# A mixture-of-experts kernel: 32 places on four column tiles for the two least used experts, wider steps, and the least used expert inside the first

## The chip, the cores and the metric

The kernel runs on one NeuronCore of a Trainium2 chip. The metric is the device time of one execution in microseconds (us), the median of several. TensorE multiplies matrices, VectorE (DVE) and ScalarE (ACT) work on the results, SyncE (SP) issues the DMA transfers, and sixteen DMA engines move data from the main memory (HBM) to the core.

## The reference

Two decoder layers on 256 tokens of width 1024, in 32-bit floats. Each layer has four kinds of attention and then a channel mixer. Layer 0 has a dense one, layer 1 one of eight experts, of which each token uses two:

```
def swiglu(x, w1, w3, w2):
    return (jax.nn.silu(x @ w1) * (x @ w3)) @ w2

logits = (xf @ w_router).astype(jnp.float32)
top_logits, top_e = lax.top_k(logits, 2)
gates = jax.nn.softmax(top_logits, axis=-1)
# each expert e: y = swiglu(its tokens, w1[e], w3[e], w2[e]), D = 1024, D_FF = 3584
# out[token] += y * gate
```

An expert has three matrices of 1024 x 3584 words, 44 MB in all; eight experts are 352 MB, and all of it has to come from HBM in each execution.

## The kernel before

The program up to about 612 us (attention, layer 0) is the same in both kernels. After it come the eight experts, one behind the other. `ranks` sorts the experts 1 to 7 by how many tokens chose them; expert 0 of the reference has rank 0, and the numbers of the others (`ids`) go to SP's registers by `values_load` (L1032), since the addresses of their weights depend on them. "Expert r" below is the one of rank r. The order is `ORDER`, (0, 7, 1, 2, 6, 3, 4, 5).

**Two kinds of expert.** `Big` (ranks 0 to 4) has 128 places for tokens. Its weights are split: `split_unit` writes the high part `whi` on ScalarE (L100) and the rest `wlo` on VectorE (L108), 1024 columns at a time with five buffers of each, and `mm3` (L134 to L136) makes three matmuls of one. `Small` (ranks 5 to 7) has 64 places and plain 32-bit matmuls of the raw weights (L1159, L1184); two matmuls of 64 columns of the array each, for different columns of the weights, fill the array.

**Loads.** `load_raw` (L84) gives a buffer of 1 MB (128 x 2048 words) from a ring of 12 with four names (raw 4, side 3, post 3, early 2) and issues a DMA for it on SP's queue. SP issues in order, so a load waits for the one before it and for the buffer's last reader, twelve loads back. An expert is 42 such loads.

**Steps.** A `Big` takes D_FF in seven steps of 512 columns, a `Small` in 1024, 1024, 1024 and 512. One step of the loop in `experts_in` is: `up` with w1; in the middle of it (after four of eight row blocks) `turn` transposes the last step's result (L1115, or L1169); silu on ScalarE (L1240); `down` of the last step with w2; `up` with w3; and on VectorE the product with the gate (L1244, `stt` below). So the last step of an expert is turned and multiplied down inside the first step of the next one. `gather` brings an expert's tokens together (L1061 and after) in the middle of the expert before, and `put_back` adds the result to `h` (L1136 for Big, L1198 for Small, L1204). PSUM has four banks for `wk` (up, turn, gather, put_back) and four for `acc` (down).

A load of 1 MB has rows in HBM of 2 KB (a step of 512 columns of w1 or w3), 4 KB (1024 columns) or 8 KB (all w2).

## Time and profile before

| | before |
|---|---|
| median of 3 runs | 1553.82 us (1552.64 to 1554.4) |
| profiled execution, its own time | 1550.38 us |
| its span | 1548.5 us |
| mean granted clock of TensorE | .993 |
| TensorE busy | 1502.4 us, 97% |
| VectorE busy | 1000.8 us, 65% |
| ScalarE busy | 842.9 us, 54% |
| read from HBM | 454.42 MB |

The span runs from the first to the last instruction on the core, the own time has some 2 us around it. The first 612 us are attention and layer 0, and the eight experts take from there to about 1505 us, so the shares of the whole span are a mean over both; the views by stage, below, tell them apart.

### The profile page before, as it was taken

The numbers are of one execution on the slowest core, as the hardware profiler recorded it, in microseconds if no ns is written. First come the engines' busy times: TensorE is split into PE (matmuls) and PEld (weight loads), VectorE is DVE, ScalarE is ACT, GpSimd is POOL, SyncE is SP. The second block draws the span as 40 slices with busy tenths as digits, with TensorE's granted clock in tenths as the row PEclk, the third lists the DMA queues.
The fourth block names the chain that finished last, engine by engine and source line by source line (L and its number), as shares of the span: only waits on it lengthen the run. The fifth ranks groups of instructions, "written<-read, shape, count | busy, mean of one in ns | idle before, by whom it ended". The sixth has DMA issues, their size and how long they took to land. (4 is left out here: it accounts for less than half of the span.)

```text
span 1548.5 us, 19459 instructions
## 1 busy us (share of the span) xinstructions
PE 1502.4 (97%) x7104; PEld 1106.6 (71%) x7104; DVE 1000.8 (65%) x1330; ACT 842.9 (54%) x1166; POOL 17.9 (1%) x20
## 2 busy tenths in 40 slices
PE   8999999999999997999999999999999999999988
PEld 6877788888788776887446888886346888885336
DVE  7676654554786767987107889886117889885016
ACT  6656544444556565876116677775025777673014
POOL 1000000000010000000000000000000000000001
PEclk9999999999999998999999999999999999999998
DMA  8553655463254642999999999999999999999993
GB/s 275 176 189 123 223 181 200 165 215 137 97 166 167 233 150 73 400 396 340 408 406 398 396 397 398 394 353 363 399 404 396 398 398 395 384 335 373 397 391 110
DMA packets 167302, 456.80 MB, mean 295 GB/s; under 512 B 10720, under 2 KB 21792, under 8 KB 151072
## 3 DMA queue, kind: packets, MB, share of 16 engines
q1 hardware_dynamic: 167200, 455.50, 78.8%
q8 instruction: 57, 0.93, 0.2%
q14 instruction: 45, 0.37, 0.1%
HBM read 454.42 MB, written 1.05 MB: 294 GB/s over the span
## 5 line engine op out<-in xcount | busy, mean ns | idle before, releaser
L108 DVE TENSOR_TENSOR wlo<-raw,whi 128x1024 fp32r<-128x1024 f32 (+1 forms) x260 | 308.6, 1214 | 77.1 <-ACT whi L100 71.7
L100 ACT ACTIVATE whi<-raw 128x1024 fp32r<-128x1024 f32 (+1 forms) x260 | 264.2, 1050 | 118.8 <-PE acc L135 66.9
L134 PE MATMUL wk<-whi,xgh 128*128 128x512 f32 x560 | 221.2, 395 | 6.7 <-ACT whi L100 6.7
L136 PE MATMUL wk<-wlo,xgh 128*128 128x512 f32 x560 | 221.7, 396 | 0.6 <-DVE wlo L108 0.6
L135 PE MATMUL wk<-whi,xgl 128*128 128x512 f32 x560 | 219.7, 392 | 0.2 <-DVE xgl L130 0.2
L108 DVE TENSOR_TENSOR wlo<-post,whi 128x1024 fp32r<-128x1024 f32 x134 | 160.9, 1221 | 21.7 <-ACT whi L100 19.7
L108 DVE TENSOR_TENSOR wlo<-side,whi 128x1024 fp32r<-128x1024 f32 x134 | 160.1, 1221 | 22.3 <-ACT whi L100 20.1
L100 ACT ACTIVATE whi<-post 128x1024 fp32r<-128x1024 f32 x134 | 137.1, 1054 | 49.9 <-PE wk L135 30.6
L134 PE MATMUL acc<-whi,gh 128*128 128x512 f32 x392 | 154.7, 395 | 4.3 <-ACT whi L100 3.3
L135 PE MATMUL acc<-whi,gl 128*128 128x512 f32 x392 | 154.7, 395 | 0.0
L1244 DVE SCALAR_TENSOR_TENSOR sl<-sl,gs,wk 128x512 f32<-128x512 f32 (+1 forms) x47 | 34.3, 730 | 182.1 <-PE wk L1159 142.1
L100 ACT ACTIVATE whi<-side 128x1024 fp32r<-128x1024 f32 x134 | 138.2, 1055 | 21.5 <-PE acc L135 11.2
L136 PE MATMUL acc<-wlo,gh 128*128 128x512 f32 x392 | 144.8, 395 | 0.1
L134 PEld LDWEIGHTS wk<-whi,xgh 128*128 128x128 f32 x560 | 105.7, 189 | 30.6 <-ACT whi L100 9.4
L136 PEld LDWEIGHTS wk<-wlo,xgh 128*128 128x128 f32 x560 | 105.8, 189 | 24.9 <-DVE wlo L108 1.6
L135 PEld LDWEIGHTS wk<-whi,xgl 128*128 128x128 f32 x560 | 105.5, 188 | 22.3 <-DVE xgl L130 0.5
L108 DVE TENSOR_TENSOR wlo<-early,whi 128x1024 fp32r<-128x1024 f32 x72 | 85.7, 1221 | 7.9 <-ACT whi L100 6.9
L134 PEld LDWEIGHTS acc<-whi,gh 128*128 128x128 f32 x392 | 73.8, 188 | 23.6 <-ACT whi L100 5.0
L134 PE MATMUL wk<-whi,hTh 128*128 128x512 f32 x224 | 88.1, 393 | 1.0 <-ACT whi L100 1.0
L136 PE MATMUL wk<-wlo,hTh 128*128 128x512 f32 x224 | 87.4, 391 | 0.1
L135 PE MATMUL wk<-whi,hTl 128*128 128x512 f32 x224 | 87.2, 390 | 0.0
L136 PEld LDWEIGHTS acc<-wlo,gh 128*128 128x128 f32 x392 | 73.6, 188 | 18.1 <-DVE wlo L108 1.0
(397 smaller groups left out, 2314.0 us busy)
## 6 DMA issues: line engine op xcount, KB each, us to landing
raw<-in_moe_w_dram SPq DMA_DIRECT2D x112, 1024.0 KB, 12.7
side<-in_moe_w_dram SPq DMA_DIRECT2D x84, 1024.0 KB, 12.8
post<-in_moe_w_dram SPq DMA_DIRECT2D x84, 1024.0 KB, 12.6
early<-in_moe_w_dram SPq DMA_DIRECT2D x56, 1024.0 KB, 12.9
raw<-in_w_in_dram SPq DMA_DIRECT2D x20, 1024.0 KB, 6.2
raw<-in_ffn_w_dram SPq DMA_DIRECT2D x19, 1024.0 KB, 5.1
post<-in_ffn_w_dram SPq DMA_DIRECT2D x14, 1024.0 KB, 5.1
side<-in_ffn_w_dram SPq DMA_DIRECT2D x9, 1024.0 KB, 5.1
```

The costliest lines, as they stand in the source:

```text
L100: nc.scalar.activation(hi, v, AF.Copy)
L108: engine.tensor_sub(lo, v, hi.bitcast(FT))
L134: nc.tensor.matmul(ps, xh, wh, start=first, stop=False)
L135: nc.tensor.matmul(ps, xl, wh, start=False, stop=False)
L136: return nc.tensor.matmul(ps, xh, wl, start=False, stop=last)
L1244: nc.vector.scalar_tensor_tensor(sl[:, :n], sl[:, :n], now.gs, ps, op0=OP.mult, op1=OP.mult)
```

## The change

The ranks 6 and 7 get 32 places and four column tiles (`q` = 4) instead of two; rank 5 keeps 64. `Big` takes 1024 columns in a step (and 512 in the last), so that `up` fills two PSUM banks and w1 and w3 are read in rows of 4 KB. `Small` takes 2048 and then 1536 columns, with rows of 8 and 6 KB; the loads of the second step are 768 KB in a buffer of 1 MB, and what remains of w2 there comes as two DMAs of 512 KB in one buffer. The loop runs over a list of pairs (expert, step), `STEPS`: the two steps of expert 7 stand behind the first of expert 0, whose other three follow. `gather` is made two steps ahead. `sl`, `gh` and `gl` are twice as wide and have one buffer in place of two.

```diff
-N_BIG = 5
-ORDER = (0, 7, 1, 2, 6, 3, 4, 5)
+PLACES = (128, 128, 128, 128, 128, 64, 32, 32)
+STEPS = [(0, 0), (7, 0), (7, 1), (0, 1), (0, 2), (0, 3)] + [
+    (r, c) for r in (1, 2, 6, 3, 4, 5) for c in range(2 if PLACES[r] < 128 else 4)]
...
-                nc.vector.tensor_scalar(room[:, N_BIG:], room[:, N_BIG:], 64.0, None, op0=OP.add)
+                for r, n in enumerate(PLACES):
+                    if n < 128:
+                        nc.vector.tensor_scalar(room[:, r:r + 1], room[:, r:r + 1], 128.0 - n, None, op0=OP.add)
...
+                cols = [(0, 1024), (1024, 1024), (2048, 1024), (3072, 512)]
+
                 def __init__(self, r, got):
                     self.r, (self.x, self.ohT, self.gs) = r, got
-                    self.cols = [(c * 512, 512) for c in range(NFC)]
                     self.y = None
+
+                def banks(self, c):
+
+                    return [512] * (self.cols[c][1] // 512)
...
-                    ps = work()
+                    ps = [work() for _ in self.banks(c)]
                     src = of_expert(name, self.r).rearrange("(k p) n -> p k n", p=128)[:, :, c0:c0 + n]
                     for k, (wh, wl) in enumerate(weights(src, [128, KD, n])):
                         if between is not None and k == 4:
                             between()
-                        mm3(ps, self.x[0][:, k], self.x[1][:, k], wh, wl, k == 0, k == KD - 1)
+                        for f, p in enumerate(ps):
+                            fs = slice(f * 512, (f + 1) * 512)
+                            mm3(p, self.x[0][:, k], self.x[1][:, k], wh[:, fs], wl[:, fs], k == 0, k == KD - 1)
...
                 def turn(self, g, c):
-                    gh = mp.tile([128, 4, 128], FR, name="gh", tag="gh", bufs=2)
-                    gl = mp.tile([128, 4, 128], FR, name="gl", tag="gl", bufs=2)
-                    p = work().rearrange("p (a b) -> p a b", a=4)
-                    for j in range(4):
-                        nc.tensor.transpose(p[:, j], g[:, 256 * (j // 2) + j % 2:256 * (j // 2 + 1):2], ident)
-                    split_sb(gh, gl, p)
+                    gh = mp.tile([128, 8, 128], FR, name="gh", tag="gh")
+                    gl = mp.tile([128, 8, 128], FR, name="gl", tag="gl")
+                    for j0 in range(0, self.cols[c][1] // 128, 4):
+                        p = work().rearrange("p (a b) -> p a b", a=4)
+                        for j in range(4):
+                            o = 128 * j0 + 256 * (j // 2)
+                            nc.tensor.transpose(p[:, j], g[:, o + j % 2:o + 256:2], ident)
+                        split_sb(gh[:, j0:j0 + 4], gl[:, j0:j0 + 4], p)
                     return gh, gl
...
+                cols = [(0, 2048), (2048, 1536)]
+
+                def __init__(self, r, got, n):
                     super().__init__(r, got)
-                    self.cols = [(0, 1024), (1024, 1024), (2048, 1024), (3072, 512)]
+                    self.n, self.q = n, 128 // n
+
+                def banks(self, c):
+                    w = self.cols[c][1] // self.q
+                    return [min(512, w - o) for o in range(0, w, 512)]
+
+                def rows(self, u):
+                    return slice(u * self.n, (u + 1) * self.n)
...
-                    ps = work()[:, :n // 2]
+                    ps = [work()[:, :w] for w in self.banks(c)]
                     src = of_expert(name, self.r).rearrange("(k p) n -> p k n", p=128)[:, :, c0:c0 + n]
-                    m = CHUNK // n
                     for k in range(KD):
-                        if k % m == 0:
-                            raw = load_raw(src[:, k:k + m], [128, m, n])
+                        raw = load_raw(src[:, k:k + 1], [128, 1, n])
                         if between is not None and k == 4:
                             between()
-                        for u in range(2):
-                            nc.tensor.matmul(ps[64 * u:64 * u + 64], self.x[:, k],
-                                             raw[:, k % m, u * (n // 2):(u + 1) * (n // 2)],
-                                             start=k == 0, stop=k == KD - 1, skip_group_check=True)
+                        for f, p in enumerate(ps):
+                            for u in range(self.q):
+                                o = u * (n // self.q) + f * 512
+                                nc.tensor.matmul(p[self.rows(u)], self.x[:, k], raw[:, 0, o:o + p.shape[1]],
+                                                 start=k == 0, stop=k == KD - 1, skip_group_check=True)
...
+                    parts = []
+                    for u in range(self.q):
+                        for a in range(w // 256):
+                            r0 = c0 + u * w + a * 256
                             raw = load_raw(wd[r0:r0 + 256].rearrange("(p j) n -> p j n", j=2), [128, 2, D])
+                            parts += [(raw[:, j], 2 * a + j, u) for j in range(2)]
+                            self.multiply(gT, c, parts)
+                        if w % 256 and u % 2:
+                            raw = load_raw(None, [128, 2, D])
                             for j in range(2):
-                                for f in range(2):
-                                    nc.tensor.matmul(self.y[64 * f:64 * f + 64], gT[:, 2 * a + j, 64 * u:64 * u + 64],
-                                                     raw[:, j, f * 512:(f + 1) * 512],
-                                                     start=(c, u, a, j) == (0, 0, 0, 0),
-                                                     stop=(c, u, a, j) == (len(self.cols) - 1, 1, n // 512 - 1, 1),
-                                                     skip_group_check=True)
+                                r0 = c0 + (u + j) * w - 128
+                                nc.sync.dma_start(raw[:, j], wd[r0:r0 + 128])
+                            parts += [(raw[:, j], w // 128 - 1, u - 1 + j) for j in range(2)]
+                            self.multiply(gT, c, parts)
+
+                def multiply(self, gT, c, parts):
+                    w = D // self.q
+                    for raw, j, u in parts:
+                        self.left = getattr(self, "left", D_FF // 128) - 1
+                        for f in range(self.q):
+                            nc.tensor.matmul(self.y[self.rows(f)], gT[:, j, self.rows(u)],
+                                             raw[:, f * w:(f + 1) * w], start=self.left == D_FF // 128 - 1,
+                                             stop=self.left == 0, skip_group_check=True)
+                    parts.clear()
...
-                                               accum_out=sums[:, t, f:f + 1])
+                                               accum_out=sums[:, t, f:f + 1] if w == 512 else None)
...
+                places = [128] * N_EXP if base else PLACES
+                seq = STEPS if base == 0 else [(r, c) for r in range(N_EXP) for c in range(len(Big.cols))]
+                first = {}
+                for s, (r, c) in enumerate(seq):
+                    first.setdefault(r, s)
+                halves_ = [0]
+                made = {}
+
+                def make(r):
+                    n = places[r]
+                    got = gather(r, n, PLACES[r] if base else 0, halves_[0])
+                    if n == 128:
+                        halves_[0] ^= 1
+                        made[r] = Big(r, got)
+                    else:
+                        made[r] = Small(r, got, n)
+
+                def make_for(s):
+                    for r, f in first.items():
+                        if f and max(f - 2, 0) == s and r not in made:
+                            make(r)
+
+                make(seq[0][0])
...
-                for place in range(N_EXP):
-                    for c in range(len(now.cols)):
-                        ps = now.up("moe_w1", c, turn_last)
-                        n = now.cols[c][1] // (2 if isinstance(now, Small) else 1)
-                        sl = mp.tile([128, 512], FT, name="sl", tag="sl", bufs=2)
-                        nc.scalar.activation(sl[:, :n], ps, AF.Silu)
-                        if before_ is not None:
-                            before_[0].down(gT, before_[1])
-                        ps = now.up("moe_w3", c)
-                        nc.vector.scalar_tensor_tensor(sl[:, :n], sl[:, :n], now.gs, ps, op0=OP.mult, op1=OP.mult)
-                        if c == len(now.cols) // 2 and place + 1 < N_EXP:
-                            then = make(place + 1)
-                        if before_ is not None:
-                            finish_last()
-                        g, before_ = sl, (now, c)
-                    now = then
+                for s, (r, c) in enumerate(seq):
+                    now = made[r]
+                    ps = now.up("moe_w1", c, turn_last)
+                    sl = mp.tile([128, 1024], FT, name="sl", tag="sl")
+                    for f, p in enumerate(ps):
+                        nc.scalar.activation(sl[:, f * 512:f * 512 + p.shape[1]], p, AF.Silu)
+                    if before_ is not None:
+                        before_[0].down(gT, before_[1])
+                    elif len(seq) > 1:
+                        make_for(s)
+                    ps = now.up("moe_w3", c)
+                    for f, p in enumerate(ps):
+                        fs = slice(f * 512, f * 512 + p.shape[1])
+                        nc.vector.scalar_tensor_tensor(sl[:, fs], sl[:, fs], now.gs, p, op0=OP.mult, op1=OP.mult)
+                    if before_ is not None:
+                        make_for(s)
+                        finish_last()
+                    g, before_ = sl, (now, c)
```

SP's queue, where the experts' numbers come to it, first before. `DMA` rows are the loads, with the buffer's name and the transfer's shape; `TENSOR_LOAD ids` fetches an expert's number.

```order
L84 DMA side<-in_moe_w_dram 128x4x512 x2
L84 DMA raw<-in_w_out_dram 128x2x1024
L84 DMA raw<-in_moe_w_dram 128x4x512
...
L84 DMA post<-in_moe_w_dram 128x4x512
L84 DMA early<-in_moe_w_dram 128x4x512
L84 DMA post<-in_moe_w_dram 128x2048
L1032 TENSOR_LOAD ids
...
L84 DMA post<-in_moe_w_dram 128x4x512
L84 DMA early<-in_moe_w_dram 128x4x512
L84 DMA raw<-in_moe_w_dram 128x2048
```

The same place after the change:

```order
L86 DMA side<-in_moe_w_dram 128x2x1024 x2
L86 DMA raw<-in_w_out_dram 128x2x1024
L86 DMA raw<-in_moe_w_dram 128x2x1024
...
L86 DMA post<-in_moe_w_dram 128x2x1024
L86 DMA early<-in_moe_w_dram 128x2x1024
L86 DMA post<-in_moe_w_dram 128x2x1024
L1037 TENSOR_LOAD ids
...
L86 DMA raw<-in_moe_w_dram 128x2048
L86 ISA
L86 DMA side<-in_moe_w_dram 128x2048
```

Ten loads of expert 0 stood ahead of the numbers, now eight of them, its whole first step up; behind them came expert 0's further weights, and now come those of expert 7.

TensorE at the first matmuls of expert 7, before: the last `up` of expert 0 (`wlo`, `xgh`), then expert 7's first loads (`xe` are its tokens), the turn of expert 0's last step (`sl`), and its last down (`acc`).

```order
L136 MATMUL wk<-wlo,xgh 128x512
L1159 MATMUL wk<-raw,xe 64x512 x4
L1159 MATMUL wk<-side,xe 64x512 x4
L1115 MATMUL wk<-ident,sl 128x128 x4
L1159 MATMUL wk<-post,xe 64x512 x4
L1159 MATMUL wk<-raw,xe 64x512 x4
L134 MATMUL acc<-whi,gh 128x512
```

And after:

```order
L138 MATMUL wk<-wlo,xgh 128x512
L1189 MATMUL wk<-raw,xe 32x512 x4
L1189 MATMUL wk<-side,xe 32x512 x4
L1189 MATMUL wk<-post,xe 32x512 x4
L1189 MATMUL wk<-early,xe 32x512 x4
L1128 MATMUL wk<-ident,sl 128x128 x8
L1189 MATMUL wk<-raw,xe 32x512 x4
L1189 MATMUL wk<-side,xe 32x512 x4
L1189 MATMUL wk<-post,xe 32x512 x4
L1189 MATMUL wk<-early,xe 32x512 x4
L136 MATMUL acc<-whi,gh 128x512
```

Before, this place is behind expert 0's seventh step, now behind its first; eight loads with four matmuls each make one `up`, and the turn takes eight transposes.

VectorE between two steps of a Big, before (512 columns, expert 0), with `stt` at L1244 and `gl` at L130:

```order
L1244 SCALAR_TENSOR_TENSOR sl<-sl,gs,wk 128x512
L108 TENSOR_TENSOR wlo<-early,whi 128x1024
L108 TENSOR_TENSOR wlo<-raw,whi 128x1024 x2
L130 TENSOR_TENSOR gl<-wk,gh 128x512
L108 TENSOR_TENSOR wlo<-side,whi 128x1024 x2
```

And after, with `stt` at L1314 and `gl` at L132:

```order
L1314 SCALAR_TENSOR_TENSOR sl<-sl,gs,wk 128x512 x2
L1252 SCALAR_TENSOR_TENSOR h,sums<-h,wk 128x512
L110 TENSOR_TENSOR wlo<-raw,whi 128x1024 x2
L110 TENSOR_TENSOR wlo<-side,whi 128x1024 x2
L110 TENSOR_TENSOR wlo<-post,whi 128x1024
L132 TENSOR_TENSOR gl<-wk,gh 128x512 x2
```

The pieces of 512 columns stand in pairs now, once in 24 split units instead of once in 12.

## Rows read from the trace of the kernel before

In the timelines L134 to L136 are the matmuls of Big, L1159 and L1184 those of Small up and down, and L1115 is the turn of Big; a row of count x8 is one load of Small, in which each matmul has two records. In the windows the columns are: stretch, its length, busy time of PE, PEld, DVE, ACT and POOL, the granted clock, the share of DMA, and GB/s.

**Rows 1.** The page of the profiled execution, its first line.
```profile
span 1548.5 us, 19459 instructions
```

**Rows 2.** Busy time in us and records (x), by stage; clock, DMA share, GB/s.
```profile
612.00:730.00 118.00, 117.77 (x535) 96.46 (x534) 104.24 (x114) 92.11 (x98) 0.00 (x0) 1.00 0.98 373
730.00:818.00 88.00, 86.11 (x427) 35.92 (x426) 14.88 (x26) 11.79 (x19) 0.00 (x0) 1.00 0.98 388
818.00:1069.00 251.00, 248.76 (x1116) 200.82 (x1116) 214.39 (x218) 179.00 (x203) 0.00 (x0) 1.00 1.02 386
1069.00:1158.00 89.00, 85.71 (x422) 35.01 (x418) 14.41 (x25) 12.80 (x20) 0.00 (x0) 1.00 1.01 395
1158.00:1411.00 253.00, 250.40 (x1114) 201.91 (x1114) 214.37 (x215) 179.85 (x204) 0.00 (x0) 0.99 1.02 383
1411.00:1505.00 94.00, 87.49 (x423) 34.06 (x422) 12.69 (x20) 10.22 (x16) 0.00 (x0) 1.00 1.01 396
...
```

**Rows 3.** The same columns for short stretches inside the stages.
```profile
840.00:860.00 20.00, 20.00 (x92) 16.50 (x91) 18.06 (x18) 15.17 (x17) 0.00 (x0) 1.00 1.04 395
1040.00:1060.00 20.00, 20.00 (x91) 16.44 (x90) 17.55 (x17) 14.95 (x17) 0.00 (x0) 1.00 0.99 369
1100.00:1120.00 20.00, 20.00 (x96) 6.81 (x94) 0.75 (x1) 1.19 (x2) 0.00 (x0) 1.00 1.02 416
1114.00:1121.00 7.00, 7.00 (x36) 2.61 (x34) 0.75 (x1) 0.60 (x1) 0.00 (x0) 1.00 1.01 421
1160.00:1180.00 20.00, 18.30 (x70) 11.54 (x69) 12.05 (x17) 11.01 (x12) 0.00 (x0) 0.91 1.03 398
```

**Rows 4.** TensorE's timeline: start, length, line, operation, count, [idle before, releaser].
```profile
817.59 0.50 PE L134 MATMUL wk<-whi,xgh 128*128 128x512 f32 x1 [1.64 <-ACT whi L100]
...
839.55 0.63 PE L1115 MATMUL wk<-ident,sl 128*128 128x128 f32 x4
...
856.56 0.63 PE L1115 MATMUL wk<-ident,sl 128*128 128x128 f32 x4
...
1068.77 1.51 PE L1159 MATMUL wk<-post,xe 128*64 128x512 f32 x6
...
1181.86 0.63 PE L1115 MATMUL wk<-ident,sl 128*128 128x128 f32 x4
```

**Rows 5.** TensorE's timeline in an expert of 64 places, a load a row.
```profile
777.49 1.94 PE L1159 MATMUL wk<-early,xe 128*64 128x512 f32 x8
779.25 1.89 PE L1159 MATMUL wk<-raw,xe 128*64 128x512 f32 x8
```

**Rows 6.** TensorE's timeline: a gather's first and last rows, a put-back's, what follows.
```profile
675.61 0.40 PE L1061 MATMUL wk<-hsh,oh 128*128 128x512 f32 x1
...
679.00 0.46 PE L1068 MATMUL wk<-ident,xs 64*128 64x64 f32 x4
...
751.13 0.50 PE L1136 MATMUL wk<-yh,ohT 128*128 128x512 f32 x1
...
753.17 1.08 PE L1159 MATMUL wk<-post,xe 128*64 128x512 f32 x4
```

**Rows 7.** Waits of SP's queue, 590 to 625 us: total, times, longest.
```profile
SPq L1032 <- DVE ids L1012: 12.7, 1, 12.7
```

**Rows 8.** DMA issues, 616:617 and 1044:1069: count, KB, us to landing.
```profile
post<-in_moe_w_dram SPq DMA_DIRECT2D x1, 1024.0 KB, 5.1
...
side<-in_moe_w_dram SPq DMA_DIRECT2D x3, 1024.0 KB, 7.2
```

**Rows 9.** Groups of VectorE's instructions, 818 to 1069: busy, mean ns, idle before.
```profile
L108 DVE TENSOR_TENSOR wlo<-post,whi 128x1024 fp32r<-128x1024 f32 x42 | 50.0, 1220 | 1.5 <-ACT whi L100 1.5
...
L1244 DVE SCALAR_TENSOR_TENSOR sl<-sl,gs,wk 128x512 f32<-128x512 f32 x14 | 10.5, 747 | 17.2 <-PE wk L136 17.2
L130 DVE TENSOR_TENSOR gl<-wk,gh 128x512 fp32r<-128x512 f32 x13 | 8.9, 685 | 0.1
```

**Rows 10.** TensorE's timeline, the matmuls on the last expert load.
```profile
1502.60 1.89 PE L1184 MATMUL acc<-early,ge 128*64 128x512 f32 x8
```

More of the change, by code (lines that the diff above doesn't have):

```diff
@@ L1038, in of_expert, with gather @@
                 return I[name][0, bass.ds(expert[r], 1)].rearrange("e k n -> (e k) n")
-            def gather(r, place, base):
-                small = r >= N_BIG
-                n = 64 if small else 128
+            def gather(r, n, off, half):
+                small = n < 128
                 sr, gr = (slot, gate) if r == 0 else (slot_r, gate_r)
@@ L1077, in gather @@
                         ins = split_sb(x[0][:, k0:k0 + 4], x[1][:, k0:k0 + 4], p)
-                    if base == 0 and r == 0:
+                    if off == 0 and r == 0:
                         table("silu_and_others", ins)
                 p = work()
-                ohT = mp.tile([128, NT, 128], FR, name="ohT", tag="ohT", bufs=2)
+                ohT = mp.tile([128, NT, 128], FR, name="ohT", tag="ohT", bufs=3)
                 for t in range(NT):
@@ L1211, in experts_in @@
             def experts_in(base, order):
-                def make(place):
-                    r = ORDER[place]
-                    return (Small if r >= N_BIG else Big)(r, gather(r, place, base))
-                now = make(0)
+                places = [128] * N_EXP if base else PLACES
[18 more added lines that the diff above has]
+                make(seq[0][0])
                 if base == 0:
```

105 lines of the change are left out of this document (58 added, 47 removed).

## The prediction

> **What bounds the kernel now.** The stage table comes first, because the share of busy time over the whole span mixes attention with the experts. From 612 us on the program is nothing but the experts' weights passing through. In each of its stages both TensorE and the DMA engines are full [rows 2]: with 128 places (818 to 1069, 1158 to 1411) TensorE works 248.76 of 251 us at a DMA share of 1.02, with 64 places (730 to 818, 1069 to 1158, 1411 to 1505) 85 to 87 us of 88 to 94. So neither engine can be relieved alone, and the question for each stage is which would end last if the other were shorter.
>
> The short stretches answer that [rows 3]. In the middle of an expert of 128 places TensorE is at 20.00 of 20 us both when DMA moves 395 GB/s and, 200 us later, at 369 GB/s and a share of .99: there TensorE sets the pace. The timeline agrees: the turns of the last result are 17.0 us apart [rows 4], one step of 512 columns, which uses 6 loads of 1 MB, so 17.0 / 6 = 2.83 us of TensorE for a load. A load of an expert of 64 places costs 1.76 us [rows 5], and DMA brings one in 1.0486 MB / 421 GB/s = 2.49 us (8 KB rows) [rows 3]. So the two kinds of stage live off one another: Big stages are paced by TensorE and let the ring of 12 fill, Small stages drain it. Where a Small stage starts, a load is on its way for 7.2 us [rows 8], that is about 2.5 of 12 buffers are in flight and some 9.5 loads lie ready.
>
> **What the change does to the durations.** Three prices follow from rows.
>
> *TensorE on 32 places.* Four column tiles instead of two: 4 matmuls of 512 columns then run side by side, half of 1.76, .88 us a load, 42 MB x .88 = 37 us less for each of the two experts, 74 us in all. The trace has no 32-place matmul; bounds are this, and that the tiles take turns (a rival below).
>
> *DMA.* 2 KB rows: at 395 GB/s a load takes 2.655 us, one in three of those has 8 KB rows, so 2 KB costs (3 x 2.655 - 2.49) / 2 = 2.74. From 416 GB/s in the same way 2.54 for 4 KB [rows 3]. Before there are 152 loads of 2 KB, 72 of 4 and 112 of 8: 878 us. After there are 20, 124 and 156, and 48 of 768 KB (6 KB rows, 3/4 of 2.49 = 1.87): 848. So DMA has 30 us less to do. The Trainium skill (DMA: Bandwidth & Descriptors, Why small descriptors are slow (HBM only)) has a fixed cost of about three cycles for a packet beside one for each 32 bytes. By that 2 KB rows would cost 3.5% more than 8 KB ones, an estimate, where the trace shows 10%; the 30 us would then be about 10.
>
> *Small edits.* The `words` tile, three additions to `room` in place of one, and the missing accumulators are pieces on DVE of under 1 us in all, behind `ids` or beside TensorE's matmuls. I cost them at nothing; without that cover it would be 1.
>
> **Front, 612 us to the turn at 839.6.** SP waits 12.7 us for the experts' numbers [rows 7], and every later load is queued behind that wait; the first lands 5.1 us after its issue at 616, that is at 621.0 [rows 8]. Now 10 loads stand ahead of the wait, after the change 8, because expert 7's addresses need it. Then come 54 up to the last that expert 7 needs (its 46, 4 of expert 0's down, 4 of expert 0's next w1): 32 of 8 KB rows, 6 of 4 KB and 16 of 768 KB, 79.7 + 15.2 + 29.9 = 124.8 us, so the last lands at 621.0 + 124.8 - 2.5 = 743.3. TensorE's work up to there is 16 loads of expert 0 (45), 42 MB of expert 7 at .88 (37), and some 6 of turns and gather: 88 of 131 us. DMA sets the end, and 43 us of TensorE are idle. These are as many as the narrow expert saves, and they can't be got back, since 26 of expert 0's 42 loads (74 us) stand behind expert 7 in TensorE's order. Then comes the return to split weights: one more landing (2.5), the split of its first half (DVE's part is 1.22 [rows 9]; the return at 817.59 shows 1.64 idle [rows 4]), and the clock, which was granted at .91 over the 20 us of such a return [rows 3], between the levels 2.4 and 1.2 GHz: .09 x 20 = 1.8. Together 5.5, to 748.8. From there to the point that is reached at 839.6 now: 26 loads of expert 0 (73.7), two put-backs (2.0 each [rows 6]), expert 1's gather (4, [rows 6]), and 5 loads of expert 1 (14.2): 844.7, against 839.6. **+5**, bounds +3 (the clock doesn't fall, no landing late) to +11 (the 6 KB rows cost what 2 KB rows do for their bytes, 16 x .18 = 3, and the return 2 more).
>
> **The Big pairs, 839.6 to 1068.8 and 1181.9 to 1411.** TensorE's matmuls are the same. With 1024 columns the pieces between steps come in pairs: two stt and two gl on DVE in one place, 2 x (.75 + .69) = 2.9 us instead of 1.4, with single sl and gh buffers. DVE has about 2 us free in 20 [rows 3], and a split unit of 1024 columns costs it 1.22, TensorE 1.42 [rows 9]. Five split buffers cover 5 x 1.42 = 7.1 us, so a bunch of 2.9 fits; it is made good at .2 us a unit, in 14 of the 24 units of a step. The bounds are 0 (covered) and the whole extra 1.4 with the silu pair's extra .6 in each of the six wide steps, plus one late unit a pair: 14. The nearest row, DVE's 18.06 of 20 with TensorE at 20.00, says covered. But a step held three of the four `wk` banks, two ups and a turn, and now two ups of two banks hold all four, so the turn waits for both stt, and they stand in DVE's queue behind splits. I put half a split unit, .7 us, on each wide step: **+4** for each pair.
>
> **Expert 6, 1068.8 to 1181.9 (113.1 now).** 52 loads (46, 2 of expert 2's last down, 4 of expert 3's w1), of which 30 have 8 KB rows, 6 have 4 KB, 16 are of 768 KB: 74.7 + 15.2 + 29.9 = 119.8 us, less the 9.5 that lie ready (23.7): 96.1. TensorE needs half of that. The last load's matmuls (.9), the return (5.5), put-back (2) and one more load of expert 3 (2.8) follow: 107.3, **-6**. Bounds: 11 loads ready, -10, and 8, -2.
>
> **Expert 5 (94 now, of it 87.49 busy).** Its places stay 64. DMA: 48 loads, 32 x 2.49 + 16 x 1.87 - 23.7 = 86, while TensorE has 87 of work; a few waits go: **-2** (-6 to 0). The last 43 us don't change.
>
> Sum: 5 + 4 - 6 + 4 - 2 = +5. The profiled execution took 1550.38 us (span 1548.5 [rows 1]), the runs' median is 3.4 above it; put on the median, 1553.8 + 5 = **1559 us**. The bounds added up give +3 + 0 - 10 + 0 - 6 = -13 and +11 + 14 - 2 + 14 + 0 = +37; all at one end is unlikely, about half of either way is -4 to +21, 1550 to 1575. The change takes 74 us off TensorE and 30 off DMA, and yet little comes out: narrow experts move the limit from TensorE to DMA, in stages where DMA has had nothing left already.
>
> **Rivals.** A change of under 0.2%, 3.1 us here, can't be told from none.
>
> *No difference.* The pairs' bunches are covered (0 instead of 8): 5 - 6 - 2 = -3, 1551. For it speaks TensorE's 20.00 of 20 with DVE at 18; against it that DVE falls behind more slowly than a stretch of 20 us shows. 0.22.
>
> *Faster: DMA sets the end everywhere.* If loads land without a pause after 621.0, the 326 left would end at 621.0 + 851 - 2.5 = 1469.5. The last matmuls on a load start at 1502.60 [rows 10], so some 33 us were lost to full buffers. After the change the remaining 340 take 848 - 20 = 828: 621 + 828 - 2.5 = 1446, with the same loss 23 earlier: 1531. For it: shares of .98 to 1.02 in every stage. Against it: TensorE's step takes 17.0 also where DMA is at .99 and 369 GB/s, and after the change 74 us less TensorE work gives a lower loss only if the ring could hold more than 12 loads. It decides if the first turn of expert 1, ten of its loads on instead of five, comes before 850 (853.8 is no gain). 0.16.
>
> *Tiles take turns.* 32 rows at a time, each matmul alone at .88: 3.5 us a load, 148 us for each narrow expert; the front ends some 60 later, expert 6 some 40: about 1655. Two tiles run at once now [rows 5], or 1.76 would be twice as much; against it nothing else. 0.04.
>
> *The clock stays low.* In 43 idle us in the front, and 45 in expert 6's stage, TensorE does little, and the granted clock fell to .91 after a stretch in which it was busier than that. If it is at 1.2 GHz for the first 11 us of Big work after either, 5.7 us more each time at most: 1565 to 1570. The Trainium skill (TensorE: Matmul & The Clock Gate, HAM oscillation — how this bites in real kernels) tells of a kernel that waits for DMA between short pieces of matmul and starts every piece at the low clock; no stretch of this trace has such waits for long. 0.08.
>
> **How the numbers follow.** My sum has 0.50, no difference 0.22, faster 0.16, the low clock 0.08, turns 0.04. The likeliest is 1559. Leaving out turns and the fully faster case, the rest lies between 1547 (no difference with expert 6's stage at its good end) and 1575 (the pairs at 1 us a place, or the low clock). Faster by over 0.2%: 0.16 and a fifth of no difference, 0.20. Same: the rest of that and the low end of my sum, 0.22. Slower: 0.58.
>
> **What would show it.** In the profile after: loads behind the ids land 2.5 us apart without a pause to about 743, and TensorE waits there on raw, side, post and early for some 40 us in all; the first matmul of expert 0's second w3 comes near 749; the first turn of expert 1 near 859. Expert 6's stage has TensorE at some 55 of 96 us. Big stages of 128 places have waits for whi or wlo of .5 us beside the silu at L1306 and the second gl; if these are nil, that +8 is wrong. The prediction is wrong altogether if TensorE's idle time before 743 is under 20 us, or if the loads land faster than 2.3 us apart.

## The result and the profile after

| | before | after |
|---|---|---|
| median of 4 runs each | 1554.11 us (1552.64 to 1558.19) | 1570.39 us (1568.79 to 1573.45) |
| profiled execution, own time | 1550.38 us | 1569.5 us |
| its span | 1548.5 us | 1567.7 us |
| mean granted clock of TensorE | .993 | .970 |
| TensorE busy | 1502.4 us | 1467.4 us |

The change makes the kernel slower: ratio 1.0103, 95% interval 1.0078 to 1.0128. TensorE has 35 us less busy time and the program takes 16 us more. The first view is the windows by stage of the kernel after (the columns are those of [rows 2]): expert 7 inside expert 0, the rest of expert 0, experts 1 and 2, expert 6, experts 3 and 4, expert 5.

```profile
641.00:748.00 107.00, 79.09 (x591) 34.30 (x583) 21.78 (x22) 19.88 (x25) 0.00 (x0) 0.86 1.02 417
748.00:847.00 99.00, 94.89 (x418) 75.89 (x419) 81.21 (x85) 70.39 (x78) 0.00 (x0) 0.97 1.02 410
847.00:1086.00 239.00, 236.06 (x1049) 189.76 (x1048) 203.53 (x210) 169.16 (x192) 0.00 (x0) 1.00 0.92 347
1086.00:1187.00 101.00, 76.16 (x596) 34.80 (x594) 22.77 (x32) 20.55 (x29) 0.00 (x0) 0.86 1.01 413
1187.00:1430.00 243.00, 239.91 (x1056) 191.72 (x1056) 203.46 (x206) 170.97 (x192) 0.00 (x0) 0.99 0.97 373
1430.00:1524.00 94.00, 88.16 (x426) 33.95 (x424) 13.10 (x21) 10.53 (x18) 0.00 (x0) 1.00 0.99 395
```

Before, TensorE and DMA were both full in every stage. Now they take turns: with the narrow experts DMA is at 413 to 417 GB/s and TensorE at 74 to 75% (even that at a clock of .86, so with less work than the busy time says); with experts 1 and 2 TensorE is at 99% and DMA falls to 347 GB/s. The freed time of either engine lies where the other has none to give. The waits of SP's queue in experts 1 and 2 (870 to 1086 us: total, times, longest) show what holds DMA there:

```profile
SPq L86 <- DVE wlo L110: 169.9, 70, 7.3
```

For 170 of 216 us the next load waits for the splits of a load twelve before: the ring is full. The same wait stood there before (840 to 1069 us):

```profile
SPq L84 <- DVE wlo L108: 148.1, 65, 7.6
```

So the wait alone tells little; how long DMA keeps its rate behind a narrow expert tells more. Here are two windows before and two after:

```profile
980.00:1000.00 20.00, 20.00 (x93) 16.58 (x92) 17.86 (x17) 13.25 (x16) 0.00 (x0) 1.00 1.03 394
1000.00:1020.00 20.00, 20.00 (x95) 16.18 (x94) 15.62 (x18) 14.15 (x18) 0.00 (x0) 1.00 1.01 370
```

```profile
847.00:861.00 14.00, 14.00 (x62) 11.17 (x60) 12.69 (x19) 8.66 (x10) 0.00 (x0) 1.00 1.01 411
861.00:880.00 19.00, 18.61 (x84) 15.13 (x84) 18.37 (x19) 15.97 (x19) 0.00 (x0) 1.00 0.92 329
```

Before, DMA is at 394 to 403 GB/s from 820 to 1000 us, some 180 us behind expert 7, and only then falls. After the change it falls 110 us behind expert 7 (751 to 861), at the start of experts 1 and 2, and from there it can only follow TensorE. The loads with wider rows come faster, 410 GB/s against 394 to 403, and a ring that fills faster is full sooner. TensorE's waits in the front (641 to 766 us) are the counterpart, 23 us of them on loads; the view's first three rows:

```profile
PE wk L136 <- ACT whi L102: 5.9, 2, 3.1
PE acc L1232 <- DMA raw<-in_moe_w_dram: 4.6, 4, 1.4
PE wk L1189 <- DMA post<-in_moe_w_dram: 4.2, 5, 1.1
...
```

To place the 19.2 us between the two profiles, TensorE's timeline of the kernel after gives the marks of [rows 4]:

```profile
614.25 0.50 PE L136 MATMUL wk<-whi,xgh 128*128 128x512 f32 x1
...
641.72 1.04 PE L1189 MATMUL wk<-side,xe 128*32 128x512 f32 x8
642.57 1.04 PE L1189 MATMUL wk<-post,xe 128*32 128x512 f32 x8
...
750.86 0.79 PE L136 MATMUL wk<-whi,xgh 128*128 128x512 f32 x1 [3.07 <-ACT whi L102]
...
861.02 1.35 PE L1128 MATMUL wk<-ident,sl 128*128 128x128 f32 x8
862.77 0.50 PE L138 MATMUL wk<-wlo,xgh 128*128 128x512 f32 x1 [0.39 <-DVE wlo L110]
...
1086.43 1.07 PE L1189 MATMUL wk<-post,xe 128*32 128x512 f32 x8
...
1204.62 1.41 PE L1128 MATMUL wk<-ident,sl 128*128 128x128 f32 x8
...
1430.16 1.08 PE L1189 MATMUL wk<-raw,xe 128*64 128x512 f32 x4
...
1523.62 0.73 PE L1245 MATMUL wk<-yh,ohT 64*128 64x512 f32 x2 [0.17 <-ACT yh L131]
```

The marks of the first turn in expert 1 and expert 3 don't stand at the same work: from there to the next narrow expert the trace before has 928 split matmuls and the one after 883, so 45 more lie ahead of the mark, 10.4 us at 0.232. With that:

| stretch | forecast | measured |
|---|---|---|
| up to the first matmul of expert 0 (612.6, 614.3) | 0 | +1.7 |
| front, to expert 1's first turn (839.6, 861.0) | +5 | 21.5 - 10.4 - 1.7 = +9.4 |
| rest of experts 1 and 2 (to 1068.8, 1086.4) | +4 | 225.4 - 229.2 + 10.4 = +6.6 |
| expert 6 (to 1181.9, 1204.6) | -6 | 118.2 - 113.1 - 10.4 = -5.3 |
| rest of 3 and 4 (to 1411.1, 1430.2) | +4 | 225.5 - 229.2 + 10.4 = +6.7 |
| expert 5 (to 1505.2, 1523.6) | -2 | 93.5 - 94.2 = -0.7 |
| tail | 0 | +0.8 |

The medians differ by 16.3, so some 3 of the 19.2 are this pair of profiles.

### The profile page after: what moved, and what is told of

Same layout as the page of the kernel before. It is cut to its first block, busy times and chain, and to the rows that moved or that the text cites. A ratio compares the mean times of both kernels' runs of the same rounds, so it can differ in the third digit from the quotient of the medians.

```text
span 1567.7 us, 19973 instructions
## 1 busy us (share of the span) xinstructions
PE 1467.4 (94%) x7330; PEld 1083.6 (69%) x7330; DVE 991.6 (63%) x1328; ACT 835.4 (53%) x1158; POOL 16.6 (1%) x20
## 5 line engine op out<-in xcount | busy, mean ns | idle before, releaser
L110 DVE TENSOR_TENSOR wlo<-raw,whi 128x1024 fp32r<-128x1024 f32 (+1 forms) x264 | 312.8, 1213 | 96.9 <-ACT whi L102 91.9
L102 ACT ACTIVATE whi<-raw 128x1024 fp32r<-128x1024 f32 (+1 forms) x264 | 269.3, 1051 | 185.0 <-DMA raw<-in_moe_w_dram 74.6
L136 PE MATMUL wk<-whi,xgh 128*128 128x512 f32 x560 | 224.1, 400 | 11.2 <-ACT whi L102 11.1
L138 PE MATMUL wk<-wlo,xgh 128*128 128x512 f32 x560 | 201.9, 402 | 3.9 <-DVE wlo L110 3.8
L136 PE MATMUL acc<-whi,gh 128*128 128x512 f32 x392 | 155.4, 396 | 8.5 <-ACT whi L102 7.5
L1314 DVE SCALAR_TENSOR_TENSOR sl<-sl,gs,wk 128x512 f32<-128x512 f32 (+2 forms) x43 | 30.2, 733 | 206.6 <-PE wk L1189 150.7
L138 PE MATMUL acc<-wlo,gh 128*128 128x512 f32 x392 | 140.2, 397 | 0.6
L136 PEld LDWEIGHTS wk<-whi,xgh 128*128 128x128 f32 x560 | 107.4, 192 | 37.8 <-ACT whi L102 14.1
L136 PEld LDWEIGHTS acc<-whi,gh 128*128 128x128 f32 x392 | 73.7, 188 | 30.7 <-ACT whi L102 13.2
L136 PE MATMUL wk<-whi,hTh 128*128 128x512 f32 x224 | 88.0, 393 | 0.9 <-ACT whi L102 0.9
L137 PEld LDWEIGHTS acc<-whi,gl 128*128 128x128 f32 x392 | 73.8, 188 | 16.1
## 6 DMA issues: line engine op xcount, KB each, us to landing
side<-in_moe_w_dram SPq DMA_DIRECT2D x73, 1024.0 KB, 10.4
```

Source lines behind the costliest of these rows:

```text
L102: nc.scalar.activation(hi, v, AF.Copy)
L110: engine.tensor_sub(lo, v, hi.bitcast(FT))
L136: nc.tensor.matmul(ps, xh, wh, start=first, stop=False)
L137: nc.tensor.matmul(ps, xl, wh, start=False, stop=False)
L138: return nc.tensor.matmul(ps, xh, wl, start=False, stop=last)
L1314: nc.vector.scalar_tensor_tensor(sl[:, fs], sl[:, fs], now.gs, p, op0=OP.mult, op1=OP.mult)
```

## Experiments

Each ran against the kernel before on the same chip; "ratio" is to it, and the kernel after stands at 1.0103 (1.0078 to 1.0128).

**1. The order undone.**

```diff
-STEPS = [(0, 0), (7, 0), (7, 1), (0, 1), (0, 2), (0, 3)] + [...]
+STEPS = [(r, c) for r in (0, 7, 1, 2, 6, 3, 4, 5) for c in range(2 if PLACES[r] < 128 else 4)]
```

> Edit: the changed kernel with expert 7 back behind all four steps of expert 0; widths and 32 places stay. Theory A (the ring: a narrow expert takes what its loads take, some 120 us, less what lies ready when it starts; in the front nothing lay ready): with three more steps of expert 0 ahead of it the ring is full when expert 7 starts, so the front goes from 12 us late to some 4 early, and the time falls by 14 to 18 us to 1553 to 1558. Theory B (the wide steps of the 128-place experts, with one buffer for each of sl, gh and gl, are what costs): 1568 to 1572, as the changed kernel. Theory C (the matmuls on four column tiles and the low clock around them cost): 1566 to 1572.

1559.08 us, ratio 1.0016 (1.0004 to 1.0028): with expert 7 back in its old place 13 us of the 16 are gone. From expert 0's first matmul to expert 6's takes 458.8 us instead of 472.1 after and 456.2 before. Theory A's ring holds, with 13 us for its 14 to 18. Theory B's wide steps have a share all the same, as run 11 shows.

**2. 64 places again.**

```diff
-PLACES = (128, 128, 128, 128, 128, 64, 32, 32)
+PLACES = (128, 128, 128, 128, 128, 64, 64, 64)
```

> Edit: the changed kernel with 64 places for ranks 6 and 7 again; order and widths stay. TensorE has some 36 us more work for each of the two. Theory A: DMA sets the end of both stages still (in the front 124 of 131 us, in expert 6's stage 86 of 96), so the 72 us cost nothing: 1567 to 1572, perhaps 2 to 4 less where the clock stays up. Theory B: the same. Theory C: the low clock and the four tiles go, 1555 to 1563. If the saved matmuls did count somewhere, 1580 or more.

1574.88 us, ratio 1.012 (1.0101 to 1.0139). In the window of expert 7 TensorE is nearly full now:

```profile
641.00:748.00 107.00, 101.02 (x486) 46.03 (x484) 24.23 (x24) 21.93 (x28) 0.00 (x0) 1.00 1.01 418
```

Yet the stage is as long: from expert 0's first matmul to the first split matmul behind expert 7 it takes 136.0 us (616.2 to 752.1) against 136.6 after the change (614.3 to 750.9). So DMA sets this stage. Theory C falls, since the clock stays at 1.00 here and nothing is gained by it. In the order of the change 72 us less work on TensorE are worth about 3 us by the ratios, which the intervals don't tell from none; in the profiles expert 6's stage is the one that gets longer, by 5.6 us to the first split matmul behind it.

**3. Steps of 512 columns for the experts of 128 places.**

```diff
-STEPS = [(0, 0), (7, 0), (7, 1), (0, 1), (0, 2), (0, 3)] + [...]
+STEPS = [(0, 0), (0, 1), (7, 0), (7, 1)] + [(0, c) for c in range(2, 7)] + [...]
...
-                cols = [(0, 1024), (1024, 1024), (2048, 1024), (3072, 512)]
+                cols = [(c * 512, 512) for c in range(NFC)]
```

> Edit: the changed kernel with the 128-place experts in seven steps of 512 columns again (2 KB rows); expert 7 stands behind the first two of them, that is behind the same 1024 columns; 32 places and the small experts' widths stay. Theory A: the front's 12 us stay, as do expert 6's 4 us of gain; the two pairs lose their 5 us each (the turn that waits for two stt): 1558 to 1563. Theory B: all 16 go, 1552 to 1556. Theory C: 1568 to 1572. If the rows of 4 KB were what kept the loss small, it is slower: 1575 or more.

1554.99 us, ratio 0.9992 (0.998 to 1.0004), 17 us less than the change on the same scale, where theory A had 10 and theory B 16. Part of the difference is in the front: two steps of 512 columns put ten loads ahead of the wait for the experts' numbers, two more than one wide step. I had estimated 5 us for these two landings; in the profiles split work is back 127.8 us after expert 0's first matmul instead of 136.6, with 24 split matmuls (5.5 us) more still to do, which leaves some 3. So this run doesn't measure the wide steps alone. It shows that in this order they cost more than their 4 KB rows brought in; what the rows are worth by themselves it doesn't show.

**4. Two wide steps of expert 0 ahead of expert 7.**

```diff
-STEPS = [(0, 0), (7, 0), (7, 1), (0, 1), (0, 2), (0, 3)] + [...]
+STEPS = [(0, 0), (0, 1), (7, 0), (7, 1), (0, 2), (0, 3)] + [...]
```

> Edit: the changed kernel with expert 7 behind two wide steps of expert 0 instead of one. Theory A (the front is paced by DMA up to expert 7's last load, and what of expert 0 stands behind it is lost time): 12 more loads come ahead (30.5 us of DMA) and 34 us less of TensorE's work stand behind, 3.5; and ten loads instead of eight stand ahead of the wait for the experts' numbers, 5: 8 to 9 us faster than the changed kernel, ratio 1.004 to 1.006. Rival (it is only that the narrow expert stands inside another): no change, 1.009 to 1.012.

1567.82 us, ratio 1.0082 (1.0056 to 1.0108): inconclusive, the interval holds both. In the profiles expert 6 begins 464.7 us after expert 0 instead of 472.1, so 7.4 came out there, nearly what A has.

**5. The turn held back.**

```diff
                         if between is not None and k == 4:
-                            between()
+                            with tc.issue_after(ins.ins):
+                                between()
...
-                            mm3(p, self.x[0][:, k], ...)
+                            ins = mm3(p, self.x[0][:, k], ...)
```

> Edit: the changed kernel, with the turn of a 128-place expert's last result held back until the fourth of eight row blocks of w1 has been multiplied, where the program text has it; in the changed kernel's order it stands 4 matmuls behind the end of w3, in the kernel before 12. The trace after has 0.171 us for a transpose (52 in a pair of experts) against 0.101 before. Theory A (of the 10 us that the two pairs lost, 7 are transposes that wait for the two stt just begun): 7 to 9 us faster than the changed kernel, ratio to before 1.004 to 1.006. Rival (VectorE's bunched pieces delay the splits, wherever the turn stands): within 2 us of the changed kernel, 1.009 to 1.012.

1579.49 us, ratio 1.0151 (1.0123 to 1.0179): slower by 7 where theory A had it faster and the rival within 2 us. The transposes do get short, but VectorE's timeline and then TensorE's at a step's end show the cost one matmul further on:

```profile
892.73 2.35 DVE L110 TENSOR_TENSOR wlo<-early,whi 128x1024 fp32r<-128x1024 f32 x2
899.39 1.41 DVE L1315 SCALAR_TENSOR_TENSOR sl<-sl,gs,wk 128x512 f32<-128x512 f32 x2 [4.31 <-PE wk L138]
900.71 2.36 DVE L110 TENSOR_TENSOR wlo<-raw,whi 128x1024 fp32r<-128x1024 f32 x2
```

```profile
901.99 0.73 PE L138 MATMUL wk<-wlo,xgh 128*128 128x512 f32 x2 [1.50 <-DVE wlo L110]
```

The two stt stand at the head of VectorE's queue and wait 4.3 us for the last matmul of w3; the next split stands behind them, though its `whi` is there. In the kernel after the transposes fill the time until it comes; with the turn held back TensorE asks for it at once and waits 1.5 us. In experts 3 and 4 its waits for `wlo` come to 7.3 us instead of 1.7. My explanation by the turn's place has fallen, and this is the next one (theory D):

**6. Two splits ahead of the stt.** `early` takes the first two units of the next w1 out of `weights`, and `up` goes on from there; `last["wlo"]` is the latest split.

```diff
                     ps = now.up("moe_w3", c)
+                    if s + 1 < len(seq) and places[seq[s + 1][0]] == 128 and places[r] == 128:
+                        made[seq[s + 1][0]].early("moe_w1", seq[s + 1][1], 2)
                     for f, p in enumerate(ps):
                         fs = slice(f * 512, f * 512 + p.shape[1])
-                        nc.vector.scalar_tensor_tensor(sl[:, fs], sl[:, fs], now.gs, p, op0=OP.mult, op1=OP.mult)
+                        with ExitStack() as behind:
+                            if getattr(made.get(seq[min(s + 1, len(seq) - 1)][0]), "it", None) is not None:
+                                behind.enter_context(tc.issue_after(last["wlo"].ins))
+                            nc.vector.scalar_tensor_tensor(sl[:, fs], sl[:, fs], now.gs, p, op0=OP.mult, op1=OP.mult)
```

> Edit: the changed kernel; the first two splits of the next step's w1 are written ahead of the two stt, and the stt are held behind them in VectorE's queue (the turn stays where the scheduler puts it). In the changed kernel the two stt wait up to 4.2 us at the head of that queue for the last matmul of w3, with split units behind them whose whi is ready; holding the turn back made it worse, since TensorE then asked for these units sooner. Theory D (the 10 us of the two pairs are VectorE's queue standing behind stt): 6 to 10 us faster than the changed kernel, ratio to before 1.004 to 1.0065. Rival (the single buffers of sl, gh and gl, or PSUM's four banks): no change, 1.009 to 1.012.

1566.77 us, ratio 1.0076 (1.0057 to 1.0095): 4 us faster than the change by the ratios, between theory D and the rival, and the two intervals overlap, so the times alone don't show a gain. The profiles do: the same 936 split matmuls of experts 3 and 4 take 240.4 us (1186.1 to 1426.5) instead of 243.1 (1187.1 to 1430.2). In experts 3 and 4 the 52 transposes take 5.0 us from start to start instead of 9.0, and of TensorE's waits for `wlo` 0.2 us is left instead of 1.7. So the place of the stt is a part of the wide steps' price, some 3 us a pair, and since the transposes got short with the same buffers and banks, these were not what held them up.

The rest, some 4 us a pair, no run has settled, but the trace after the change shows a second place of the same kind, on ScalarE. Here are its timeline and then TensorE's, behind the end of a w1:

```profile
907.60 1.09 ACT L1306 ACTIVATE sl<-wk 128x512 f32<-128x512 f32 x2 [3.16 <-PE wk L138]
908.57 1.06 ACT L102 ACTIVATE whi<-raw 128x1024 fp32r<-128x1024 f32 x1
```

```profile
909.69 0.50 PE L136 MATMUL acc<-whi,gh 128*128 128x512 f32 x1 [0.26 <-ACT whi L102]
```

Two silus wait 3.2 us for the last matmul of w1 (at most 1.4 before, and one silu), the next `whi` comes behind them, and TensorE's down runs into it. In experts 3 and 4 that happens once in each of three steps, 1.0 us of waiting; from start to start the down matmuls there lose some 3 us against their usual 0.23 each, about as much in run 6, and nothing with steps of 512 columns (run 11). No run moved the silus, so this is read from the trace and not shown by an experiment.

**7. The spread order.** Nothing but the list: a step of a narrow expert behind each expert of 128 places.

```diff
-STEPS = [(0, 0), (7, 0), (7, 1), (0, 1), (0, 2), (0, 3)] + [...]
+STEPS = [(0, 0), (0, 1), (0, 2), (0, 3), (7, 0), (1, 0), (1, 1), (1, 2), (1, 3), (7, 1),
+         (2, 0), (2, 1), (2, 2), (2, 3), (6, 0), (3, 0), (3, 1), (3, 2), (3, 3), (6, 1),
+         (4, 0), (4, 1), (4, 2), (4, 3), (5, 0), (5, 1)]
```

> Edit: the changed kernel with another list of steps and nothing else: expert 0, the first step of expert 7, expert 1, the second of 7, expert 2, first of 6, expert 3, second of 6, expert 4, expert 5. Theory A: what the changed kernel loses is DMA's time while the ring is full in the long runs of 128-place experts; an expert of them gives some 20 us of lead, a ring holds 24, and one step of a narrow expert uses 27 to 36, so the ring is never full for long and loads land without a pause from 623 on. 828 us of DMA then end near 1455, and the rest of the program takes 46 more: 1505 to 1520. Theory B: the wide steps are as many, 1565 to 1572. Theory C: four returns from narrow steps instead of two, 5 us each: 1575 to 1582.

1533.97 us, ratio 0.9853 (0.983 to 0.9875): 22 us under the kernel before and by the ratios some 39 under the change, with the same work in another order. Of the 39, run 1 had 13 by moving expert 7 alone, so some 25 come from the spreading. The numbers of theories B and C fall. Theory A's 1505 to 1520 is at least 14 us too low: loads don't land without a pause. The window of all experts in this order, and after it that of the change:

```profile
640.00:1480.00 840.00, 796.24 (x4121) 559.91 (x4119) 546.66 (x573) 461.95 (x527) 0.00 (x0) 0.98 0.99 397
```

```profile
640.00:1520.00 880.00, 812.03 (x4120) 559.78 (x4119) 546.18 (x574) 460.44 (x528) 0.00 (x0) 0.96 0.97 383
```

397 GB/s instead of 383, against 410 to 417 in stretches where DMA never waits. The gain is in the 128-place experts, where both engines are full at once now, as here in expert 2:

```profile
948.60:1062.90 114.30, 113.14 (x501) 89.81 (x502) 93.63 (x95) 78.20 (x87) 0.00 (x0) 0.99 1.02 412
```

TensorE is as busy as in experts 1 and 2 after the change, and DMA moves 412 GB/s beside it instead of 347. The narrow step ahead of each such expert has taken loads out of the ring, and there is room for new ones.

**8. The spread order with 64 places.** The edits of 2 and 7.

> Edit: the spread list of steps with 64 places for ranks 6 and 7, 36 us more of TensorE for each. Theory A (in the spread order loads and matmuls are both near their limit, TensorE idle some 50 us of the 870 with the experts): of the 72 us half can't be hidden, ratio 1.00 to 1.02 against 0.985 for the spread order, whereas in the changed order they cost 3 us. Rival (DMA alone sets the end in the spread order): under 6 us more, below 0.99.

1573.58 us, ratio 1.0129 (1.0095 to 1.0163): the 32 places that are worth some 3 us, if any, in the order of the change are worth 42 here. Theory A holds. TensorE's busy time shows why:

```profile
640.00:1520.00 880.00, 857.17 (x3871) 573.13 (x3872) 546.07 (x574) 461.51 (x532) 0.00 (x0) 1.00 0.96 377
```

857 of 880 us: with 64 places TensorE is the bound again, so in the spread order the two engines do share it, which neither price alone would show.

**9 and 10. The spread order with the turn held back, and with the splits ahead of stt.** The edits of 5 and 6 on 7.

> Edit: the spread list of steps and the turn held back, both. Theory A (TensorE and DMA share the bound there): 3 to 8 us faster than the spread order, ratio 0.980 to 0.983. Rival (DMA alone sets the end there): as the spread order, 0.985.

1539.18 us, ratio 0.9891 (0.9862 to 0.9919): not faster but some 6 us slower than the spread order, the way that run 5 went; theory A is missed here too.

> Edit: the spread list of steps and the splits ahead of stt, both. Theory D with A: there TensorE and DMA share the bound (64 places cost 42 us in that order), so most of the 10 us and of expert 0's come out: 5 to 10 us faster than the spread order, ratio 0.978 to 0.982. Rival (the splits are not it): 0.985.

1526.35 us, ratio 0.9831 (0.9809 to 0.9853): the lowest ratio of all, 26 us under the kernel before. The gain over the spread order, 3 us by the ratios, is under what the intervals tell apart, so theory D's 5 to 10 are not shown.

**11. Only the narrow experts.** The order of the kernel before and seven steps of 512 columns; what stays are 32 places and the small experts' wide rows.

> Edit: the changed kernel with the order of the kernel before (expert 7 behind all of expert 0) and with seven steps of 512 columns for the experts of 128 places; what stays of the change are 32 places and the small experts' rows of 8 and 6 KB. Theory A: experts 7 and 6 each gain the 4 us that the changed kernel's expert 6 gained, and nothing is lost: 6 to 12 us under the kernel before, ratio 0.992 to 0.996. Rival (four column tiles, the low clock and the two returns cost as much as they save): 0.998 or more.

1548.8 us, ratio 0.9969 (0.9957 to 0.9981): 5 us faster than before, between theory A's 0.992 to 0.996 and the rival's 0.998, and the interval reaches both. This part of the change is a gain by itself, if a smaller one than theory A had.

From this run two ways of single edits lead to the change, and together they divide the 16 us. Wide steps first: 0.9969 becomes 1.0016 (run 1), 7 us, and expert 7 inside expert 0 then adds 13. Expert 7 first, behind two steps of 512 columns: 0.9969 becomes 0.9992 (run 3), 4 us, and the wide steps then add 17. Each of these has an interval of 2 to 4 us. So the narrow experts bring 5, wide steps alone cost 7 and the place alone 4, and some 10 us come only from both together. Of these, some 3 are the two loads fewer ahead of the wait for the experts' numbers (run 3); the rest no run divides.

**12. The spread order with steps of 512 columns.** The edits of 3 and 7.

> Edit: the spread list of steps with seven steps of 512 columns (2 KB rows) for the experts of 128 places. In the changed order that made the kernel 16 us faster, so there the 4 KB rows were worth nothing. Theory A: in the spread order loads land with hardly a pause, so 120 loads that take 0.2 us more each, 24 us, count; 8 to 10 us of TensorE's bunching and the like come back: 8 to 16 us slower than the spread order, ratio 0.990 to 0.996. Rival (wide steps cost in any order, and DMA has room): faster than the spread order, 0.975 to 0.982.

1530.74 us, ratio 0.9854 (0.9825 to 0.9883), as the spread order to within the intervals. Neither theory had it. A window (640 to 1470 us) shows DMA at a share of 1.02:

```profile
640.00:1470.00 830.00, 785.82 (x4105) 560.40 (x4105) 549.18 (x573) 460.86 (x527) 0.00 (x0) 0.98 1.02 400
```

It agrees with a price of the 2 KB rows on DMA and one of the wide steps on TensorE that are about equal here, but the two weren't separated.

## Why the prediction was right, and where its sizes were off

**The bound.** Right: expert 7's time in the front is its loads' time. Run 2 shows it, since 22 us more of TensorE's time there change nothing, and run 1 shows that with the wide steps the place costs 13 us. One of the signs that I had named came out much weaker, though. TensorE was to wait some 40 us for loads before 743; it waits 20.7, and its idle time is 25.7 us:

```profile
614.00:743.00 129.00, 103.35 (x684) 54.73 (x682) 42.89 (x62) 36.56 (x45) 0.00 (x0) 0.88 0.97 400
```

My 88 us of work were at the full clock; the granted clock was .88 on average, and at that the same work takes longer and fills much of the idle time. Expert 6's stage is the same: TensorE was to work some 55 of 96 us, and it is busy for 75.7 of 97.6.

**The front, +5, measured +9.4.** The right mechanism, with two terms mis-sized inside the bounds of 3 to 11. The first is the loads' end. The last load that expert 7 needs was to land at 743.3, and TensorE's wait for it ends at 747.15:

```profile
747.15 0.64 PE L1232 MATMUL acc<-side,ge 128*32 128x256 f32 x8 [0.64 <-DMA side<-in_moe_w_dram]
```

Of these 3.8 us 1.7 are the later start of expert 0, a row of its own in the table; the other 2.1 are loads that began and ran a little later than in my sum. The return's wait itself is as forecast: 2.5 + 1.2 = 3.7, and from 747.15 to 750.86 it is 3.7. (My 748.8 had 1.8 for the clock in it, which falls behind the start of the split work.) The second term is that clock. The windows after the change:

```profile
689.00:708.00 19.00, 13.45 (x128) 4.49 (x128) 0.00 (x0) 0.00 (x0) 0.00 (x0) 0.65 1.01 419
708.00:723.00 15.00, 9.18 (x64) 1.42 (x64) 0.46 (x1) 0.00 (x0) 0.00 (x0) 0.77 1.02 416
723.00:751.00 28.00, 19.43 (x148) 13.17 (x148) 10.01 (x11) 11.01 (x14) 0.00 (x0) 0.92 1.02 414
751.00:766.00 15.00, 14.96 (x60) 11.51 (x60) 10.67 (x11) 10.79 (x11) 0.00 (x0) 0.81 1.02 409
...
750.00:755.00 5.00, 4.10 (x9) 2.80 (x10) 3.98 (x4) 3.92 (x5) 0.00 (x0) 0.50 1.02 405
755.00:760.00 5.00, 5.00 (x20) 4.04 (x19) 4.59 (x5) 3.89 (x5) 0.00 (x0) 0.82 1.03 409
760.00:765.00 5.00, 5.00 (x25) 3.87 (x23) 1.26 (x2) 3.98 (x4) 0.00 (x0) 1.00 1.03 410
```

While TensorE waits for loads the granted clock is .65 to .92 on average, between its levels of 1.2 and 2.4 GHz, which costs nothing there: run 2, at 1.00, is no earlier. The first split work behind it still runs at the lower level, and the clock is back at 1.00 in the window from 760; over the 15 us from 751 it is .81, .19 x 15 = 2.9 us, where I had 1.8 from another return. The Trainium skill (TensorE: Matmul & The Clock Gate, HAM oscillation — how this bites in real kernels) tells of the low clock behind waits for DMA, and this trace agrees, with .81 in those 15 us. The loads' 2.1 and the clock's 1.1 are three quarters of the 4.4 that the front was off. The last 1.2 are in TensorE's 110 us behind the return, in which its waits for other engines come to 1.1 us and its 20 transposes take 0.9 us longer than at the 0.101 of the kernel before. So the bunched pieces of expert 0's wide steps can account for that rest, but not for the whole miss.

That the clock stays low was a rival at 0.08 with at most 5.7 us a return. Its 1565 to 1570 lies nearer to the measured time than my 1559, but that is luck: of the 11 us at 1.2 GHz in it, which no row had shown, the trace has about half, and the 2.9 us are a part of the loss, not the whole.

**The pairs, +4 each, measured +6.6 and +6.7.** Within 0 to 14, and the +8 for both is near the 7 us that runs 11 and 1 give for the wide steps in the old order, but the reason given was turned round, so the size is luck. I wrote that the stt stand in VectorE's queue behind splits and the turn waits for them. The runs show splits that stand behind stt. The rows of VectorE's waits (847 to 1086 us after, 840 to 1069 before: total, times, longest) have it:

```profile
DVE sl L1314 <- PE wk L138: 15.5, 7, 4.2
```

```profile
DVE sl L1244 <- PE wk L136: 16.9, 12, 2.6
```

The total is alike; one wait is up to 4.2 us instead of 2.6, and two stt follow it instead of one. Runs 5 and 6 settle the direction, and in the profiles some 3 of the 6.7 us; that the turn waits for banks is not borne out by run 6. That the silu pair does the same on ScalarE was in my upper bound, as .6 us of its own work and not as a wait that others stand behind.

**Expert 6, -6, measured -5.3; expert 5, -2, measured -0.7.** Right, inside the bounds. Run 11, where expert 7 stands where such a gain can be had as well, gives 5 us for all the narrow experts together, so in that order a narrow expert brings less than the 6.

**The rivals.** That DMA sets the end everywhere falls with 347 GB/s in experts 1 and 2. That tiles take turns falls with a load of 32 places every 0.85 us (641.72 to 642.57 above), half of the 1.76 in [rows 5]; I had .88. No difference falls with the interval.

**The sum.** 1559 was forecast and 1570.39 measured, inside 1547 to 1575. Between the two profiles the sum was off by 14 (19.2 against 5): 4 in the front, 5 in the pairs, 2 in experts 6 and 5, and 2.5 ahead of and behind the experts. Between the medians it was 11. The 30 us of DMA that the wide rows save, and the 74 of TensorE that 32 places save, came to little for the reason given: most of it lay where its engine was not the one waited for. What the narrow experts do bring, 5 us in run 11, the wide steps and expert 7's place took back.

## What to carry to other kernels

Where two kinds of stage are bound by different engines and a ring of buffers joins them, the ring's depth in time (here 12 loads of about 2.5 us, some 30 us) limits how long a stretch of one kind the other can pay for. Work saved on one engine then counts where the kinds are mixed in portions of about that size: the same work took 1570 us with the narrow expert in one piece where nothing lay ready, and 1534 with its steps spread. Two sizes of portion were tried, so the limit itself is worked out and not measured. And before an elementwise piece is doubled, look at what stands behind it in its engine's queue while it waits for its input.

## What the runs showed of the hardware that I had not expected

Matmuls on four column tiles of 32 reached their full share in w1: 0.85 us for 1 MB of weights against 1.76 on two of 64. The granted clock fell to .65 in 19 us in which TensorE's busy time was still 13.45, its matmuls coming in short groups between loads, while with 64 places, 101 of 107 us busy, it stayed at 1.00.
